# A fixed order at the begin of the joint stage, half 0's root one output tile earlier, and the last adaLN dots as GpSimd products summed by ScalarE

## The chip, the cores and the metric

The kernel runs on one core of a Trainium2 chip. The metric is the device time of one execution in microseconds, as a median of runs. TensorE is called PE in the profile, VectorE DVE, ScalarE ACT and GpSimd POOL; SP is the engine that issues most of the loads.

## The reference

One layer of a bidirectional encoder with 1024 positions and a width of 1024 (8 heads and 2 key heads of 64, window 128, 8 gMLP groups, feed-forward width 2816). Cut to what matters:

```python
mod = silu(c) @ w_ada + b_ada                 # adaLN
sh1, sc1, gt1, sh2, sc2, gt2 = split(mod, 6)
h = rmsnorm(x, norm1_g) * (1 + sc1) + sh1
u, v, q, k, va, gate_a, gate_b = split(h @ w_in)
v = rmsnorm(gelu(v), v_gain)
a_out = (gelu(u) * (w_s @ v + b_s)) @ w_a      # per chunk of 128 positions, per group
b_out = window_attention(q, k, va) @ w_b       # |t-s| <= 128, ALiBi, a sink per head
merged = sigmoid(gate_a) * a_out + sigmoid(gate_b) * b_out
x = x + gt1 * (merged @ w_o)
h2 = rmsnorm(x, norm2_g) * (1 + sc2) + sh2
f_gate, f_up = split(h2 @ w_ffn_in)
return x + gt2 * ((silu(f_gate) * f_up) @ w_ffn_out)
```

## The kernel before

Activations are kept with the width on the 128 partitions and positions along the row. The positions are two halves of 512. Every large product is made of three matmuls of rounded operands (high by high, low by high, high by low): `mm3` (L164) issues them, `unit` (L156) turns a raw weight tile into its high part `wh` (a cast on ACT) and its low part `wl` (a subtraction on DVE or POOL). One output tile of 128x512 takes 24 matmuls of 512 columns where the inner size is 1024. All operations go through a recording class whose call is L76, so every row of the profile has that line; `load` (L137) issues on SP and `store` (L140) on POOL. PE, DVE, ACT and POOL each run their own instructions in the order in which they stand; a scheduler chooses that order, except where `in_order[0]` is set: such instructions keep the order of the program (`tc.keep_in_program_order`). In feed-forward the order is all by hand (`tc.manual_schedule`).

The stages, in the order of time:

1. `half(hf)` (L732) for each half: q, k and v, the windowed attention, and the gMLP. The loop over `gp` (L1105) multiplies the position-mixing matrices with v into PSUM banks, and a `scalar_tensor_tensor` on DVE evicts each group into `ut` as u * (mixed + bias). Sixteen transposes of `ut` and a split into high and low parts (`gH`, `gL`) follow. The loop `for d in range(KT)` (L1157, eight output tiles) projects both branches by W_ab; for d below 2 the banks are multiplied with the gates right away, for the others stored.
2. In half 1 the same loop runs jobs ahead of the joint stage: `block_sums(k, part)` (L606) builds, from the normalised x of both halves, the blocks B11, B21, B22 and their sums and differences T1 to T4. The chunks it reads are a0, a1 (tiles `hs`) and b0, b1 (tiles `xs`), loaded by `block_load` (L586), b1 by an addition on POOL.
3. The joint stage, `for d in range(2, KT)` (L1239): the gates of both halves together by seven products in place of eight, `gate_step(d, i)` and `gate_evict(d, i)` with i from 0 to 6. Sums of weights are made by `gate_sums`, high and low parts by `gate_prep_a`, `_b`, `_c`, of which the last two return functions that issue the low part later. `held_projection` (L1211) is the last projection of half 1, kept back. `ada_half` (L542) computes one adaLN column as two dots of 512 on DVE. The order in this loop is the program's.
4. The output projection `for hf in range(2): for d in range(KT)` (L1344): W_o's product, an eviction to x1 = product * gt1 + x, the sum of squares `ss`, and a store of x1 to DRAM. In half 1, `col_rstd(sums[0], ...)` (L288) multiplies the squares of half 0 with ones on PE (tiles `at<-ones,ss`) and takes the root, `spread` (L295) spreads it over the partitions, and `mod2(i)` (L1336) loads x1 of half 0 back and makes the normalised, modulated h2 of tile i (tiles `mid` and `h`), which feed-forward multiplies first.
5. Feed-forward: groups f of hidden tiles, seven products each in later groups (step i), then the output products. `gain_dots(f, i)` (L1707) computes the eight last adaLN columns (gt2) from group EARLY = 6 on: it loads a row of w_ada, and two `scalar_tensor_tensor` with an accumulated sum on DVE make the dot.

The profile's tile names are those of the program without their numbers: `mm` and `at` are banks, `t` short-lived tiles, `raw` weights as loaded, `j` and `mid` the blocks' high and low parts among others.

## Time and profile before

| what | value |
|---|---|
| median of 3 runs | 1268.25 us (1266.0 to 1270.06) |
| the profiled execution | 1264.82 us |
| its span on the core | 1263.0 us |
| mean granted PE clock in it | 0.994 of full speed |

The span is the time from the first to the last instruction that the profile shows; 1.8 us of the execution lie outside it. In the timeline a row is: start, duration of the whole row, engine, line, operation, tile written and tiles read, shape, count, and in brackets the idle time of the engine before it and who ended it. In the table of windows a row holds the window, its length, the busy time and count of PE, PEld (the loading of weights into PE), DVE, ACT and POOL, then PE's granted clock, the busy share of the DMA engines and the GB/s. In the list of waits: the engine and tile that waited, what for, the sum, the number and the longest.

### The profile page before, as it was taken

The page shows a single profiled execution, that of the slowest core. Times are in us where ns is not written, and L with a number is a line of the kernel's source. Part 1 is how long each engine was busy: PE and PEld are TensorE (multiplying, and loading weights), DVE is VectorE, ACT ScalarE, POOL GpSimd, SP SyncE. Part 2 cuts the span into 40 slices and gives each one's busy share as a digit, 9 for nine tenths or more (in the row PEclk, how much of TensorE's full clock was granted, in tenths as well). Part 3 has the DMA queues.
Part 4 walks back from the last instruction along what each step waited for, and adds up shares of the span by engine and source line. Part 5 has one row for each costly group of instructions (what it writes and reads, how often), then busy time and mean ns, then how long its engine had stood idle before and what let it go on. Part 6 is the DMA issues. An engine that isn't in the chain of part 4 may idle for free.

```text
span 1263.0 us, 15661 instructions
## 1 busy us (share of the span) xinstructions
PE 1226.5 (97%) x5634; PEld 1013.4 (80%) x5634; DVE 917.3 (73%) x1548; ACT 577.7 (46%) x938; POOL 176.7 (14%) x218
## 2 busy tenths in 40 slices
PE   5999999999989999999899999999999999999998
PEld 4888888888877887788788887888788887888887
DVE  8998883588887799866798766777676676455646
ACT  5477864367866333434454332333333334443442
POOL 1223430013342000211100000000010000010001
PEclk9999999999999999999899999999999999999999
DMA  9722168421146466677702454565644549785542
GB/s 363 265 100 67 68 202 299 132 84 51 63 160 236 159 201 233 237 246 243 256 35 100 152 215 159 191 233 200 233 171 181 182 167 347 284 326 192 191 159 100
DMA packets 78688, 236.29 MB, mean 187 GB/s; under 512 B 9361, under 2 KB 9361, under 8 KB 72594
## 3 DMA queue, kind: packets, MB, share of 16 engines
q1 hardware_dynamic: 57602, 146.67, 33.3%
q0 software_dynamic: 17552, 82.32, 18.2%
q10 hardware_dynamic: 3456, 6.29, 1.3%
q8 instruction: 44, 0.72, 0.2%
q14 instruction: 34, 0.28, 0.1%
HBM read 177.58 MB, written 57.67 MB: 186 GB/s over the span
## 4 chain that ended last, share of the span: by engine, by line
PE 58%; issue 16%; DVE 13%; DMA 8%; ACT 4%; POOL 1%; SPq 0%; ACTq 0%; POOLq 0%; DVEq 0%
PE mm L76 31%; PE at L76 27%; DVE mid L76 4%; DVE wl L76 3%; DMA hs<-in_w_ada_dram 2%; DMA wS<-wo 2%; DMA wo<-in_w_out_dram 1%; ACT wh L76 1%; DVE hs L76 1%; DVE xs L76 1%; DMA mid<-in_w_ada_dram 1%; DMA hs<-x1d 1%; DVE t L76 1%; DVE ws L76 1%; ACT lb L76 1%
## 5 line engine op out<-in xcount | busy, mean ns | idle before, releaser
L76 DVE TENSOR_TENSOR wl<-raw,wh 128x1024 fp32r<-128x1024 f32 x141 | 171.9, 1221 | 90.8 <-ACT wh L76 88.6
L76 ACT CAST wh<-raw 128x1024 fp32r<-128x1024 f32 x155 | 162.4, 1051 | 149.9 <-PE at L76 47.7
L76 PE MATMUL mm<-mid,wh 128*128 128x512 f32 x696 | 215.5, 390 | 0.7 <-DVE mid L76 0.4
L76 PEld LDWEIGHTS mm<-mid,wh 128*128 128x128 f32 x696 | 130.3, 188 | 29.3 <-DVE mid L76 1.1
L76 PE MATMUL at<-j,wh 128*128 128x512 f32 x464 | 143.0, 389 | 0.0
L76 PE MATMUL mm<-mid,wl 128*128 128x512 f32 x348 | 135.4, 390 | 0.0
L76 PE MATMUL mm<-wh,h 128*128 128x512 f32 x384 | 128.9, 397 | 2.8 <-ACT h L76 2.8
L76 PEld LDWEIGHTS at<-j,wh 128*128 128x128 f32 x464 | 87.0, 188 | 18.2 <-ACT xs L76 0.2
L76 PE MATMUL at<-h,wh 128*128 128x512 f32 x288 | 91.3, 397 | 3.0 <-ACT h L76 2.8
L76 DVE TENSOR_TENSOR wl<-ws,wh 128x1024 fp32r<-128x1024 f32 (+1 forms) x55 | 62.0, 1128 | 43.0 <-ACT wh L76 43.0
L76 PE MATMUL mm<-j,wh 128*128 128x512 f32 x288 | 89.9, 394 | 0.9 <-ACT wh L76 0.9
L76 PE MATMUL at<-j,wl 128*128 128x512 f32 x232 | 90.4, 390 | 0.2 <-DVE wl L76 0.2
L76 PEld LDWEIGHTS mm<-wh,h 128*128 128x128 f32 x384 | 71.2, 188 | 17.9 <-ACT h L76 4.1
L76 PE MATMUL mm<-h,wh 128*128 128x512 f32 x272 | 84.6, 392 | 0.0
L76 ACT CAST wh<-ws 128x1024 fp32r<-128x1024 f32 (+1 forms) x55 | 53.6, 974 | 63.8 <-DVE ws L76 54.3
L76 PEld LDWEIGHTS mm<-mid,wl 128*128 128x128 f32 x348 | 65.3, 188 | 14.1 <-DVE wl L76 0.3
L76 PE MATMUL mm<-wl,h 128*128 128x512 f32 x192 | 75.1, 391 | 0.4 <-DVE wl L76 0.4
L76 PEld LDWEIGHTS at<-h,wh 128*128 128x128 f32 x288 | 54.8, 191 | 15.9 <-ACT h L76 3.2
L76 PEld LDWEIGHTS mm<-j,wh 128*128 128x128 f32 x288 | 54.3, 189 | 12.4 <-ACT wh L76 1.3
L76 ACT ACTIVATE xs<-xs 128x512 f32<-128x512 f32 x21 | 13.3, 633 | 105.3 <-DVE xs L76 105.3
L76 DVE TENSOR_TENSOR ol<-raw,oh 128x1024 fp32r<-128x1024 f32 x30 | 36.7, 1224 | 32.6 <-ACT oh L76 32.5
L76 PEld LDWEIGHTS mm<-h,wh 128*128 128x128 f32 x272 | 50.6, 188 | 10.4
(279 smaller groups left out, 2580.3 us busy)
## 6 DMA issues: line engine op xcount, KB each, us to landing
raw<-in_w_gate_dram SPq DMA_DIRECT2D x28, 512.0 KB, 4.0
tA<-hid POOLq DMA_DIRECT2D x11, 1024.0 KB, 5.0
tB<-hid POOLq DMA_DIRECT2D x11, 1024.0 KB, 5.0
wo<-in_w_out_dram POOLq DMA_DIRECT2D x22, 512.0 KB, 6.1
wS<-wo POOLq DMA_DIRECT2D x11, 1024.0 KB, 5.3
raw<-wS SPq DMA_DIRECT2D x44, 256.0 KB, 3.0
raw<-tB SPq DMA_DIRECT2D x44, 256.0 KB, 3.4
raw<-in_w_out_dram SPq DMA_DIRECT2D x33, 256.0 KB, 5.1
```

The costliest lines, as they stand in the source:

```text
L76: ins = f(*args, **kw)
```

## The change

Six edits:

- **The gMLP's evictions** of half 1 keep the program's order, and so do the projections of tiles 6 and 7 and the jobs behind tiles 0, 6 and 7 of half 1.
- **The blocks**: the negation of B22 goes from the first part of `block_sums` to the end of the second. `block_sums(3, 1)` is no job any more: it stands in the joint stage. At d = 2 the order there becomes step 0, its eviction, `held_projection`, `block_sums(3, 1)`, step 1; it was step 0, eviction, step 1, `held_projection`.
- **`ada_half`** in the joint stage stands behind the low part of `gate_prep_c` in the step's first third, and no longer at the step's end.
- **Half 0's root** stands at the begin of output tile 1 of half 1 and not of tile 2, `spread` at the begin of tile 2 and not within tile 3; `mod2` runs at tiles 2 to 7 as 0; 1; 2, 3; 4; 5, 6; 7 where it ran at 3 to 7 as 0, 1; 2; 3, 4; 5; 6 and 7 behind the last eviction.
- **`gain_dots`**: each of the sixteen fused products with sum on DVE becomes a `tensor_tensor` on POOL (steps 2 and 4) and an activation with `accum_out` on ACT at the next odd step; the row is loaded at step 6 and no longer at 5.
- The store of silu(c) is written behind block 5 of attention and not behind block 0; on POOL it stands in the same place in both kernels.

DVE at the end of half 1, before. `mid_2667` is `ut`, `at_3656` to `at_3683` the gMLP's banks, `mid_2671` is `gL`; `xs_3747`, `xs_3743`, `hs_3745` are the block's chunks b1, b0, a0; `t_760` and `t_761` the gates of projection tile 0; `wl_3802` the low part of W_ab's weights of tile 2 (two stretches, the eviction of the transposes between them left out):

```order
L76 TENSOR_TENSOR xs_3620<-at_3615,xs_3620 64x512
L76 TENSOR_TENSOR xs_3747<-xs_3747,xs_3743 128x512
L76 SCALAR_TENSOR_TENSOR mid_2667<-at_3656,cc,mid_2667 128x4x64 x2
L76 SCALAR_TENSOR_TENSOR mid_2667<-at_3665,cc,mid_2667 128x4x64 x2
L76 SCALAR_TENSOR_TENSOR mid_2667<-at_3674,cc,mid_2667 128x4x64 x2
L76 SCALAR_TENSOR_TENSOR mid_2667<-at_3683,cc,mid_2667 128x4x64 x2
```

```order
L76 TENSOR_TENSOR xs_3743<-xs_3743,hs_3745 128x512
L76 SCALAR_TENSOR_TENSOR t_760_3692<-t_760_3692,mm_3751 128x512
L76 SCALAR_TENSOR_TENSOR j_3784<-xs_3747,nsh,j_3783 128x512
L76 SCALAR_TENSOR_TENSOR mid_3838<-hs_3745,mod,mid_3837 128x512
L76 TENSOR_TENSOR xs_3747<-xs_3747,hs_3745 128x512
L76 SCALAR_TENSOR_TENSOR mid_3841<-hs_3749,mod,mid_3840 128x512
L76 SCALAR_TENSOR_TENSOR t_761_3694<-t_761_3694,mm_3765 128x512
L76 TENSOR_TENSOR j_3788<-xs_3743,j_3787 128x512
L76 TENSOR_TENSOR t_760_3692<-t_760_3692,t_761_3694 128x512
L76 TENSOR_TENSOR j_3793<-xs_3747,j_3792 128x512
L76 TENSOR_TENSOR wl_3802<-raw_3734,wh_3801 128x1024
```

DVE at the same place with the change (`wl_3800` is that low part), from the gMLP's evictions to the weights, without the eviction of the transposes:

```order
L76 TENSOR_TENSOR xs_3620<-at_3615,xs_3620 64x512
L76 SCALAR_TENSOR_TENSOR mid_2667<-at_3656,cc,mid_2667 128x4x64 x2
L76 SCALAR_TENSOR_TENSOR mid_2667<-at_3665,cc,mid_2667 128x4x64 x2
L76 SCALAR_TENSOR_TENSOR mid_2667<-at_3674,cc,mid_2667 128x4x64 x2
L76 SCALAR_TENSOR_TENSOR mid_2667<-at_3683,cc,mid_2667 128x4x64 x2
```

```order
L76 SCALAR_TENSOR_TENSOR t_760_3692<-t_760_3692,mm_3751 128x512
L76 SCALAR_TENSOR_TENSOR t_761_3694<-t_761_3694,mm_3765 128x512
L76 TENSOR_TENSOR t_760_3692<-t_760_3692,t_761_3694 128x512
L76 TENSOR_SCALAR nsh<-mod 128x8
L76 TENSOR_TENSOR xs_3747<-xs_3747,xs_3743 128x512
L76 TENSOR_TENSOR xs_3743<-xs_3743,hs_3745 128x512
L76 SCALAR_TENSOR_TENSOR j_3784<-xs_3747,nsh,j_3783 128x512
L76 TENSOR_TENSOR xs_3747<-xs_3747,hs_3745 128x512
L76 TENSOR_TENSOR hs_3749<-xs_3747,hs_3749 128x512
L76 TENSOR_TENSOR j_3788<-xs_3743,j_3787 128x512
L76 TENSOR_TENSOR j_3793<-xs_3747,j_3792 128x512
L76 TENSOR_TENSOR wl_3800<-raw_3734,wh_3799 128x1024
```

The sum of b1 and b0 moved from ahead of the four pairs of evictions to a place behind the gates of tile 0, and with it the whole block, so that the gates of tile 0 now stand ahead of every sum of it and all of it ahead of the weights.

DVE at the begin of the joint stage, before: the block's last sums, the weights' sums (`raw`), and the low part of step 1's weights (`wl_4121`):

```order
L76 TENSOR_TENSOR xs_4057<-xs_4057,hs_4052 128x512
L76 TENSOR_TENSOR j_3788<-xs_4004,j_3787 128x512
L76 TENSOR_TENSOR raw_4013<-raw_4013,t_841_4070 128x512
L76 TENSOR_TENSOR j_3793<-xs_4057,j_3792 128x512
L76 TENSOR_TENSOR raw_4013<-raw_4013 128x512
L76 TENSOR_TENSOR hs_4060<-xs_4057,hs_4060 128x512
L76 TENSOR_TENSOR wl_4121<-raw_4015,wh_4120 128x1024
L76 TENSOR_TENSOR t_849_4124<-t_841_4070,t_848_4123 128x512
L76 SCALAR_TENSOR_TENSOR h_3849<-hs_4060,nsh,h_3848 128x512
```

The same place with the change (`wl_4119` is step 1's low part):

```order
L76 TENSOR_TENSOR xs_4055<-xs_4055,hs_4050 128x512
L76 TENSOR_TENSOR j_3788<-xs_4004,j_3787 128x512
L76 TENSOR_TENSOR j_3793<-xs_4055,j_3792 128x512
L76 TENSOR_TENSOR wl_4119<-raw_4013,wh_4118 128x1024
L76 TENSOR_TENSOR raw_4011<-raw_4011,t_841_4070 128x512
L76 TENSOR_TENSOR raw_4011<-raw_4011 128x512
L76 TENSOR_TENSOR t_849_4122<-t_841_4070,t_848_4121 128x512
L76 TENSOR_TENSOR hs_4058<-xs_4055,hs_4058 128x512
L76 SCALAR_TENSOR_TENSOR h_3847<-hs_4058,nsh,h_3846 128x512
```

The low part of step 1's weights moved up by three rows, ahead of two sums of weights and the last block's sum. On PE the 12 matmuls of `held_projection` stand between steps 0 and 1 with the change, and behind step 1 before.

PE in the output projection of half 1, before: `mm_5461` is output tile 0, `mm_5497` tile 1, `mm_5539` tile 2, `at_5540` the product of ones with half 0's squares `ss_5077`:

```order
L76 MATMUL mm_5497<-j_5118,wh_5455 128x512
L76 MATMUL mm_5497<-j_5117,wl_5456 128x512
L76 MATMUL at_5540<-ones,ss_5077 128x1 x4
L76 MATMUL mm_5539<-j_5115,wh_5491 128x512
L76 MATMUL mm_5539<-j_5116,wh_5491 128x512
```

The same with the change (the product is `at_5498`):

```order
L76 MATMUL mm_5461<-j_5118,wh_5399 128x512
L76 MATMUL mm_5461<-j_5117,wl_5400 128x512
L76 MATMUL at_5498<-ones,ss_5077 128x1 x4
L76 MATMUL mm_5497<-j_5115,wh_5455 128x512
L76 MATMUL mm_5497<-j_5116,wh_5455 128x512
```

The four matmuls with ones moved from behind tile 1 to behind tile 0, 24 matmuls earlier. On DVE and ACT the sums of squares of half 0 keep their order.

```diff
--- before.py
+++ after.py
@@ -581,7 +581,7 @@
     nsh = const.tile([P, 16], F32, tag="nsh", name="nsh")[:, :8]
     blk = {}
 
-    chunk = {}
+    chunk, kinds = {}, []
 
     def block_load(k, name):
         if k < 4:
@@ -629,8 +629,6 @@
             low1()
             block_load(k + 1, "b0")
             low2()
-            for x in blk["B22"]:
-                A.activation(x[:, k, :], x[:, k, :].bitcast(F32), AF.Copy, scale=-1.0)
             return
         if k < 3:
             low = b11()
@@ -643,6 +641,8 @@
         block_load(k + 1, "b1")
         low()
         block_load(k + 1, "a1")
+        for x in blk["B22"]:
+            A.activation(x[:, k, :], x[:, k, :].bitcast(F32), AF.Copy, scale=-1.0)
 
     raws, gunits, acc, held = {}, {}, {}, []
 
@@ -1060,7 +1060,7 @@
                 x_square(s + 1)
             if hf == 0 and s == 7:
                 x_rstd()
-            if hf == 0 and s == 0:
+            if hf == 0 and s == 5:
                 store(silu_d, silu_c)
             normalise(sc[0], sc[2], den)
             if s == 0:
@@ -1110,6 +1110,7 @@
                 wc = slice(g * P, (g + 1) * P)
                 mm3(pg[:, e * 256 : (e + 1) * 256], (ws[0][:, wc], ws[1][:, wc]),
                     (vH[:, g, :], vL[:, g, :]), True, True)
+            in_order[0] = hf == 1
             for e in range(2):
                 g = 2 * gp + e
                 uu = ut[:, :, g * HD : (g + 1) * HD]
@@ -1117,6 +1118,7 @@
                     out=uu, in0=pg[:, e * 256 : (e + 1) * 256].rearrange("p (n d) -> p n d", d=HD),
                     scalar=bsT[:, g : g + 1], in1=uu, op0=ALU.add, op1=ALU.mult,
                 )
+            in_order[0] = False
         def gate_act(pg):
             sg = tmp()
             A.activation(sg, pg, AF.Tanh, scale=0.5)
@@ -1147,15 +1149,15 @@
         else:
             apool_ctx.close()
             jpools.append(ffn_ctx.enter_context(pool("j", 6, reuse_waits="tile")))
-            kinds = (lambda: midt(F32R, 4)), (lambda: jt(F32R, 4)), hid
+            kinds[:] = (lambda: midt(F32R, 4)), (lambda: jt(F32R, 4)), hid
             blk["B22"] = (hH[1], hL[1])
             for x in ("b0", "a0", "b1", "a1"):
                 block_load(0, x)
             jobs.extend((2 * k + p, lambda k=k, p=p: block_sums(k, p, kinds))
-                        for k in range(4) for p in range(2))
+                        for k in range(4) for p in range(2) if k + p < 4)
 
         for d in range(KT):
-            in_order[0] = d < 2
+            in_order[0] = d < 2 or hf == 1 and d > 5
             if 0 < d < KT - 1:
                 wab.append(unit(None, V, abr.pop(0)))
                 if d + 2 + hf < KT:
@@ -1194,9 +1196,10 @@
             if d < 2:
                 V.tensor_tensor(ms[0], ms[0], ms[1], op=ALU.add)
                 store(md[hf][d], ms[0])
-            in_order[0] = False
+            in_order[0] = hf == 1 and (d < 1 or d > 5)
             while jobs and jobs[0][0] <= d:
                 jobs.pop(0)[1]()
+            in_order[0] = False
             if hf == 0:
                 ada_next(d < 1)
                 if d > 5:
@@ -1240,8 +1243,9 @@
         if d == 2:
             gate_step(d, 0)
             gate_evict(d, 0)
+            held_projection()
+            block_sums(3, 1, kinds)
             gate_step(d, 1)
-            held_projection()
             low_c = gate_prep_c(d)
             gate_evict(d, 1)
             low_c()
@@ -1261,7 +1265,6 @@
             gate_evict(d, 5)
             low_b()
             low_s()
-            ada_half("hs")
             continue
         gate_step(d, 0)
         gate_evict(d, 0)
@@ -1269,6 +1272,7 @@
         low_c = gate_prep_c(d)
         gate_evict(d - 1, 6)
         low_c()
+        ada_half("hs" if not last else None)
         if not last:
             gate_load(d + 1)
         gate_step(d, 1)
@@ -1315,7 +1319,6 @@
             if d in (3, 4, 5):
                 ada_half("hs")
             low_s()
-            ada_half("hs" if d < KT - 2 else None)
     in_order[0] = False
     for k in (4, 5, 7):
         m_split(m0, k)
@@ -1357,15 +1360,15 @@
             load(xk, x_rows(hf, d))
             pw = mm_bank()
             for k in range(KT):
+                if hf == 1 and (d, k) == (1, 0):
+                    col_rstd(sums[0], NT, rcol[2])
                 if hf == 1 and (d, k) == (2, 0):
-                    col_rstd(sums[0], NT, rcol[2])
-                if hf == 1 and (d, k) == (3, 3):
                     rb = spread(rcol[2], NT)
                 kc = slice(k * P, (k + 1) * P)
                 mm3(pw, (wo[0][:, kc], wo[1][:, kc]),
                     (m[k // 4][0][:, k % 4, :], m[k // 4][1][:, k % 4, :]), k == 0, k == KT - 1)
             if hf == 1:
-                for i in {3: (0, 1), 4: (2,), 5: (3, 4), 6: (5,), 7: (6,)}.get(d, ()):
+                for i in {2: (0,), 3: (1,), 4: (2, 3), 5: (4,), 6: (5, 6), 7: (7,)}.get(d, ()):
                     mod2(i)
             x1 = tmp() if hf == 0 else x1B[d // 4][:, d % 4, :]
             V.scalar_tensor_tensor(out=x1, in0=pw, scalar=mod[:, GT1 + d : GT1 + d + 1], in1=xk,
@@ -1385,7 +1388,6 @@
                 if 0 < d < 7:
                     ada_next(False)
             if hf == 1 and d == KT - 1:
-                mod2(d)
                 early.append(unit(None, V, raw1))
         in_order[0] = False
         sums.append(ss)
@@ -1702,29 +1704,29 @@
                             for x in "hl"]
             split2(raws[n], *ready[n])
 
-    again = []
+    again, dots = [], []
 
     def gain_dots(f, i):
         if f == EARLY and i == 0:
             again.extend(stream("hs") for _ in range(2))
             for j in range(2):
                 dma(again[j], silu_d[:, j * 512 : (j + 1) * 512])
-        if not ada_queue:
-            return
-        if f >= EARLY and i == 5:
+        if f >= EARLY and ada_queue and i == 6:
             again[2:] = [tmp(), tmp()]
             for j in range(2):
                 dma(again[2 + j], w_ada2[ada_queue[0][0] - GT1][:, j * 512 : (j + 1) * 512])
-        if f > EARLY and i in (3, 4):
-            j = int(i == 4)
+        if dots and i % 2:
+            dots.pop(0)()
+        if f > EARLY and ada_queue and i in (2, 4):
+            j = i // 2 - 1
             col = ada_queue[0][0]
             part = sm(16, "part")[:, :1]
-            V.scalar_tensor_tensor(out=again[2 + j], in0=again[2 + j], scalar=1.0, in1=again[j],
-                                   op0=ALU.mult, op1=ALU.mult,
-                                   accum_out=part if j else acc_mod[:, col : col + 1])
+            row = again[2 + j]
+            G.tensor_tensor(row, row, again[j], op=ALU.mult)
+            dots.append(lambda: A.activation(row, row, AF.Copy,
+                                             accum_out=part if j else acc_mod[:, col : col + 1]))
             if j:
-                added(acc_mod[:, col : col + 1], part)
-                ada_end(col)
+                dots.append(lambda: (added(acc_mod[:, col : col + 1], part), ada_end(col)))
                 ada_queue.pop(0)
 
     with tc.manual_schedule():
```

## The prediction

> **What bounds the kernel now.** I read the page's busy shares first, then the waits of the matmul engine alone, in two windows, and then the timeline around each wait that is long enough to matter.
>
> ```profile
> span 1263.0 us, 15661 instructions
> PE 1226.5 (97%) x5634; PEld 1013.4 (80%) x5634; DVE 917.3 (73%) x1548; ACT 577.7 (46%) x938; POOL 176.7 (14%) x218
> ```
>
> TensorE (PE) is busy for 1226.5 of 1263.0 us, and the change leaves the number of matmuls as it is. So what can be won is the 36.5 us in which PE stands still, and the time in which it runs at a lower clock. Where it waits, between 340 and 640 us and then after 640 us (line, what it waits for: sum, times, longest, in us):
>
> ```profile
> PE at L76 <- DVE mid L76: 4.8, 2, 4.0
> PE at L76 <- ACT h L76: 2.8, 1, 2.8
> PE mm L76 <- DVE wl L76: 1.7, 2, 1.3
> PE mm L76 <- ACT wh L76: 0.9, 1, 0.9
> ```
>
> ```profile
> PE mm L76 <- DVE wl L76: 1.6, 1, 1.6
> PE at L76 <- DVE xs L76: 0.8, 1, 0.8
> ```
>
> Four waits carry the first window, and three places hold them: the transposes behind the gMLP gate of half 1, the joint stage's begin, and the begin of feed-forward. After 640 us there is little to win. Each of the three places is followed by a window in which the granted clock (the column PEclk, behind the five engines) is 0.50. The windows below are 350 to 357, 401 to 408, 620 to 627 us, two of feed-forward, and the stretch of half 1's projections.
>
> ```profile
> 350.28:353.69 3.41, 0.00 (x0) 0.00 (x0) 3.38 (x3) 1.67 (x3) 3.41 (x2) 1.00 0.08 18
> 353.69:357.10 3.41, 3.11 (x15) 3.07 (x16) 3.41 (x9) 1.46 (x4) 1.46 (x1) 0.50 0.61 196
> 401.48:404.90 3.42, 1.72 (x6) 1.15 (x7) 3.42 (x6) 2.57 (x5) 0.00 (x0) 1.00 0.64 264
> 404.90:408.30 3.40, 3.40 (x9) 2.64 (x9) 0.67 (x2) 0.00 (x0) 0.00 (x0) 0.50 0.81 259
> ...
> 619.90:626.70 6.80, 6.21 (x18) 4.93 (x19) 4.15 (x6) 5.75 (x7) 1.04 (x1) 0.50 0.43 155
> 710.00:830.00 120.00, 118.04 (x518) 96.78 (x517) 82.57 (x128) 40.57 (x56) 8.82 (x17) 1.00 0.55 200
> 830.00:960.00 130.00, 129.21 (x570) 106.68 (x569) 95.69 (x151) 43.20 (x60) 11.22 (x21) 1.00 0.57 204
> 353.00:403.00 50.00, 47.77 (x210) 39.42 (x210) 45.90 (x68) 34.87 (x55) 15.18 (x16) 0.97 0.61 205
> ```
>
> The window behind a wait runs 3.4 us at half clock, so it does 1.7 us of work; a wait that goes takes these 1.7 us with it, and a new wait may bring them.
>
> **A, the gate's evictions in written order.**
>
> ```profile
> 350.12 2.82 DVE L76 TENSOR_TENSOR xs<-xs,xs 128x512 f32<-128x512 f32 x1 [3.50 <-POOL xs L76]
> 352.97 3.23 DVE L76 SCALAR_TENSOR_TENSOR mid<-at,cc,mid 128x256 f32<-128x256 f32 x8
> 350.04 5.12 POOL L76 TENSOR_TENSOR wl<-raw,wh 128x1024 fp32r<-128x1024 f32 x2
> 353.99 3.45 PE L76 MATMUL at<-ident,mid 128*128 128x128 f32 x16 [4.05 <-DVE mid L76]
> ```
>
> VectorE (DVE) is idle for 3.50 us on a sum of a joint-stage block whose other operand GpSimd (POOL) writes; that sum then takes 2.82 us; only then come the eight evictions, while PE waits 4.05 us for them. In the new order the block's sum stands behind the evictions. The banks come until 349.95 (353.99 less 4.05); the last pair then needs 2 x 0.40 us (3.23 over 8), so 0.85 us of the wait stays. Gone: 4.05 - 0.85 + 1.7 (the half clock) = 4.9, and 0.3 of the eight being begun while banks still come: **-5.2 us**, bounds -3.2 (the clock falls all the same) and -5.75 (all goes).
>
> The same rows show why the sum was slow: 2.82 us beside POOL's subtraction, where one of this size takes 0.68 alone (below), while the evictions, with one operand from a bank, ran 0.40 apart beside the same subtraction. The Trainium skill, "SBUF — State Buffer", section "Who interferes with whom", has it as an exclusive lock on a pair of ports, taken by a DVE instruction with two inputs from SBUF against a GpSimd one that reads SBUF; these rows agree. It speaks against the last part of the change, F.
>
> **B, a new wait two projection tiles later.** In the fixed order DVE has to take the gates of projection tile 0 (two products with a bank, and their sum) before it goes to the first block's sums. Tile 0 is 24 matmuls at 0.227 us, 5.44 us, as its neighbours are.
>
> ```profile
> 357.20 0.72 PE L76 MATMUL mm<-mid,wh 128*128 128x512 f32 x2
> 402.05 0.68 DVE L76 TENSOR_TENSOR hs<-xs,hs 128x512 f32<-128x512 f32 x1
> 402.65 1.21 DVE L76 TENSOR_TENSOR wl<-raw,wh 128x1024 fp32r<-128x1024 f32 x1
> 571.29 0.74 DVE L76 SCALAR_TENSOR_TENSOR t<-mm,mod,xs 128x512 f32<-128x512 f32 x1
> 572.96 1.05 ACT L76 CAST wh<-raw 128x1024 fp32r<-128x1024 f32 x1 [2.92 <-DMA raw<-in_w_o_dram]
> 573.91 0.63 ACT L76 ACTIVATE t<-t 128x512 f32<-128x512 f32 x1
> ```
>
> Tile 0 begins at 357.20 now; without A's 5.2 us it begins at 352.0 and ends at 357.4. Behind that end stand on DVE a product of 0.74 (as at 571.29), a sum and two block sums 0.60 apart (402.05 to 402.65), a product of 0.74 and another sum; the block's cast on ScalarE (ACT), taken like the 0.63 row, and the weights' cast of 1.05 follow behind it: 357.4 + 0.74 + 3 x 0.60 + 0.74 + 0.60 + 0.63 = 361.9 for the begin of the weights' cast. One short instruction and the handovers between the two engines are not in this; I put them at 0.1 to 0.7 in all, an estimate, so the cast of tile 2's weights ends at 363.1 to 363.7. PE, after tiles 0 and 1, wants it at 352.0 + 2 x 5.44 = 362.9. Then four matmuls (0.9 us) need the cast alone; DVE's subtraction of 1.21 us has one more sum before it and ends about 0.6 us behind them. I take 0.8 + 0.6, since every handover adds: **+1.4 us**, bounds 0 (the weights' cast slips in earlier) and +3.1 (the clock falls too).
>
> On that clock there is a rule. In 401.48 to 404.90 PE did 1.72 of 3.42 us, with waits of 0.88 and 1.29, and got 0.50 in the next window. The Trainium skill, "TensorE: Matmul & The Clock Gate", section "HAM oscillation — how this bites in real kernels", asks only that no gap without work be over about 3.4 us. By that rule B would stay at 1.4; by the row it could be 3.1. The row decides that shorter gaps can do it, and 3.1 stays as the bound.
>
> **C, the joint stage's begin.**
>
> ```profile
> 401.90 0.74 PE L76 MATMUL mm<-j,wh 128*128 128x512 f32 x2 [0.88 <-ACT wh L76]
> 403.92 0.50 PE L76 MATMUL mm<-j,wl 128*128 128x512 f32 x1 [1.29 <-DVE wl L76]
> ```
>
> PE waits 0.88 and 1.29 us for step 1's weights, and the half clock of 404.90 to 408.30 adds 1.7. The change puts the 12 matmuls of the held projection ahead of step 1, 12 x 0.227 = 2.72 us of cover, and lets the low part of the weights go three rows earlier on DVE, 3 x 0.60 = 1.8 us. Against it: PE arrives 3.8 us earlier (A and B), and DVE, 45.90 of 50 us busy between 353 and 403, has to come forward as well. It gets 2.14 (2.82 less 0.68) from A's sum, and it has 4.1 us of idle time, of which I count about 0.4: PE gains 1.3 us on it. The cover of 4.5 less 1.3 is over the 2.17 needed. The two dots that stand later or earlier by three rows in every joint step (1.4 us beside steps without a wait of PE) are part of this order and cost nothing. **-3.9 us**, bounds 0 and -3.9.
>
> **D, half 0's root at tile 1.** The matmuls of ones against the sum of squares stand behind tile 0 instead of behind tile 1.
>
> ```profile
> 571.57 0.61 PE L76 MATMUL mm<-j,wh 128*128 128x512 f32 x2
> 577.02 0.95 PE L76 MATMUL at<-ones,ss 128*128 128x1 f32 x8
> 574.04 1.23 DVE L76 TENSOR_TENSOR wl<-raw,wh 128x1024 fp32r<-128x1024 f32 x1 [2.01 <-ACT wh L76]
> 575.18 0.69 DVE L76 TENSOR_TENSOR ss<-ss,t 128x512 f32<-128x512 f32 x1
> ```
>
> Now PE comes to them at 577.02, when the last sum has been there since 575.87 (575.18 + 0.69). One tile earlier it comes at 571.57, and the sum isn't earlier: the last square (573.91) stands on ACT behind the weights' cast, which waits 2.92 us for a transfer, and the last addition on DVE behind the subtraction of 574.04, which waits for that cast. Neither engine's order around it changes. All of tile 1 is queued behind the waiting matmul: 575.87 - 571.57 = 4.3 us, and the half clock after it 1.7: **+6.0 us**. Bounds: without the detour through the weights the sum would be there at 571.29 + 0.74 + 0.63 + 0.69 = 573.35, 1.8 us late, so +1.8; a second half-clock window gives +7.7. The root itself and the spread of it, a tile earlier too, have nobody waiting for them.
>
> **E, half 0's modulation earlier.**
>
> ```profile
> 616.97 0.50 PE L76 MATMUL at<-h,wh 128*128 128x512 f32 x1 [0.26 <-DVE h L76]
> 620.49 1.58 PE L76 MATMUL at<-h,wh 128*128 128x512 f32 x2 [2.79 <-ACT h L76]
> 619.72 0.72 ACT L76 ACTIVATE h<-mid,mod 128x512 fp32r<-128x512 f32 x1 [1.42 <-DVE mid L76]
> ```
>
> Feed-forward's first product waits for the last two tiles of the normalised half 0: 0.26 + 2.79 us, and 6.8 us at half clock follow, in which PE is busy for 6.21, worth 3.1. The last tile is now issued before the eviction of output tile 7 and not after it, and the others a tile earlier, which puts 5.44 us of matmuls ahead of the need. Half a microsecond I leave for the last one: 3.05 + 3.1 - 0.5: **-5.6 us**, bounds -1.0 (DVE, which now has two such tiles beside one output tile, is late) and -6.2.
>
> **F, the dots.** Sixteen fused products with sums leave DVE; sixteen products come to POOL and sixteen sums to ACT.
>
> ```profile
> L76 DVE SCALAR_TENSOR_TENSOR t<-t,hs 128x512 f32<-128x512 f32 x16 | 10.9, 683 | 0.0
> L76 DVE DVE_READ_ACCUMULATOR t<-t,hs 128x1 f32 x16 | 1.3, 82 | 0.0
> ```
>
> ```profile
> 348.79 1.30 POOL L76 TENSOR_TENSOR xs<-h,h 128x512 f32<-128x512 f32 x1
> 776.75 0.69 DVE L76 TENSOR_TENSOR hid<-hid 128x512 f32<-128x512 f32 x1 [3.81 <-DMA wS<-wo]
> ```
>
> DVE loses 10.9 + 1.3 = 12.2 us of work. Almost none of it is on the path: PE is busy 118.04 of 120 and 129.21 of 130 us, and the one longer wait of PE there, the 1.6 us for wl above, stands behind a DVE sum that waits 3.81 us for a transfer. POOL gets 16 x 1.30 = 20.8 us, 0.53 us more per dot than DVE is freed of (1.30 less 0.77), if each product shuts DVE out for its whole length; DVE has 37.4 us without work in the first of these windows and 34.3 in the second, which hide that. ACT's sums, of about the length of the 0.63 row, fall on an engine at 34% (40.57 of 120). The store of silu(c) moves in the code only. **-1.0 us**, bounds -2.4 (the waits over 640 us of the second waits fence) and +3.
>
> **The sum.** -5.2 + 1.4 - 3.9 + 6.0 - 5.6 - 1.0 = -8.3. The profiled execution took 1264.82 us (1.8 outside its span): 1256.5. The median of the runs, 1268.25, stands 3.4 us above that execution, so on its scale I forecast 1259.9, say **1260**.
>
> **Rivals.** *R1, the root's wait is mostly hidden*: the last square overtakes the cast, D is +1.8 and not +6.0: 1260 - 4.2 = 1256. For it speaks that ACT only waits for a transfer; against it, that the order on ACT and DVE there is unchanged. *R2, DVE is the bound between 353 and 403*: at 92% busy it does not come forward, C is 0, and 1.3 us of A comes back as a longer wait at the joint stage's begin: 1260 + 5.2 = 1265. For it: the share. Against it: the idle 3.50 us and the stretched 2.82 us both lie ahead of this stretch, so DVE starts it earlier. *R3, slower: POOL's products shut out DVE's subtractions in feed-forward.* All sixteen on the path, at 1.30 us, give +20.8 where I have -1.0: 1260 + 21.8 = 1282. The kernel is slower beyond 0.3% from 1272.1 - 1261 = 11.1 us of it, 9 of the 16 products. For it: the 2.82 us of A. Against it: a step of 12 matmuls is 2.72 us, in which DVE works 69% or 1.87 us, less the dot that leaves; 1.87 - 0.77 + 1.30 = 2.40 still fits. The change may also not do what it says at E, where a late DVE leaves 4.6 of the 5.6 us: 1264.6.
>
> **How the numbers follow.** Forecast 0.48, R1 0.15, R2 with E's failure 0.23, R3 0.14. What a measurement can tell from no change is 0.3%, 3.8 us: faster is below 1264.4, slower above 1272.1. Forecast and R1 are faster nearly whole, and a little of R2: 0.65. The rest of R2 and the forecast's upper end: 0.22. R3 with the upper bounds of B and D: 0.13. The range runs from R1 with the better bounds of A, B, E and F (1252) to R2 with the upper bounds of B and D and a little of F's (1270); it leaves out R3 and little else.
>
> **What would show it.** A: no wait near 350 us, and no window of 0.50. B: a wait of PE for tile 2's cast or low part about 10 us later. C: step 1's matmuls without a wait behind the held projection's. D: `at<-ones,ss` with some 4 us of idle time for DVE's ss and a 0.50 window after it; without it R1 holds. E: no wait for h at feed-forward's first product. F: DVE subtractions of 1.21 us stretched beyond 2 us beside POOL's products, and new waits for wl after 800 us, would be R3. The forecast is wrong if the mean clock falls below 0.994, or if waits for DVE appear between 360 and 403 us that I do not have.

## The result and the profile after

The changed kernel takes 1265.72 us (median of 20 runs, 1260.78 to 1269.63); the kernel before, run beside it, 1266.37 us (20 runs, 1263.6 to 1270.34). The ratio is 0.9992, 95% interval 0.9981 to 1.0004: no difference. The forecast was 1260 us and faster; the time lies inside the range of 1252 to 1270 us, but the gain is not there.

The profiled execution must be read with one caution. It took 1269.63 us, the slowest of its 20 runs, while that of the kernel before, 1264.82 us, lies 1.5 us below its median. The two traces differ by 4.9 us of span where the medians differ by 0.65, so a place is judged below by several traces of the same order of work.

The page of the changed kernel, the span and the busy shares:

```profile
span 1267.9 us, 15678 instructions
PE 1228.1 (97%) x5634; PEld 1013.0 (80%) x5634; DVE 919.5 (73%) x1516; ACT 586.0 (46%) x970; POOL 198.9 (16%) x234
```

TensorE does the same matmuls. Its waits in the changed kernel, from 340 to 420 us, 420 to 560, 560 to 640, and 640 to 1000 (one fence each; sum, times, longest):

```profile
PE mm L76 <- ACT wh L76: 0.6, 1, 0.6
PE mm L76 <- POOL wl L76: 0.5, 1, 0.5
PE at L76 <- DVE wl L76: 0.5, 1, 0.5
PE mm L76 <- DVE wl L76: 0.3, 1, 0.3
```

```profile
PE at L76 <- DVE mid L76: 4.1, 3, 1.5
```

```profile
PE at L76 <- DVE ss L76: 5.3, 2, 4.2
```

```profile
PE mm L76 <- ACT xs L76: 3.6, 3, 1.7
PE mm L76 <- DVE wl L76: 2.9, 2, 2.3
```

The waits of 4.0, 1.3 and 0.9 us around 350 and 402 us are gone, as forecast, and so is the 2.8 us for h. Three groups stand in their place: 4.1 us in the joint stage, where the kernel before has 1.1; 5.3 us for sums of squares, where it has none; and 6.5 us in feed-forward, where it has 2.8. The rows of B's wait, of the first wait in the joint stage, of the root and of the begin of feed-forward:

```profile
363.20 1.20 PE L76 MATMUL mm<-mid,wh 128*128 128x512 f32 x4 [0.61 <-ACT wh L76]
364.66 0.50 PE L76 MATMUL mm<-mid,wl 128*128 128x512 f32 x1 [0.27 <-DVE wl L76]
451.01 2.33 PE L76 MATMUL at<-j,t 128*128 128x512 f32 x9 [1.44 <-DVE mid L76]
573.32 1.59 PE L76 MATMUL at<-ones,ss 128*128 128x1 f32 x8 [4.20 <-DVE ss L76]
623.25 1.02 PE L76 MATMUL at<-ones,ss 128*128 128x1 f32 x8 [1.06 <-DVE ss L76]
```

The windows of the changed kernel (gate, joint stage, root, begin of feed-forward, feed-forward):

```profile
349.00:352.40 3.40, 2.85 (x20) 2.20 (x19) 2.28 (x6) 3.40 (x7) 3.40 (x3) 1.00 0.02 5
352.40:355.80 3.40, 3.40 (x16) 2.80 (x15) 3.22 (x6) 1.44 (x3) 1.77 (x1) 1.00 0.71 186
440.00:500.00 60.00, 55.93 (x243) 44.81 (x242) 53.32 (x98) 19.74 (x27) 4.85 (x9) 1.00 0.64 217
573.30:576.70 3.40, 3.38 (x13) 3.00 (x14) 2.13 (x4) 2.52 (x3) 2.05 (x2) 0.55 0.85 286
576.70:580.10 3.40, 3.40 (x10) 2.63 (x9) 1.07 (x1) 0.00 (x0) 0.49 (x1) 0.50 0.61 233
620.00:627.00 7.00, 5.93 (x26) 4.56 (x25) 5.13 (x7) 5.08 (x8) 1.58 (x2) 0.85 0.23 80
710.00:830.00 120.00, 115.17 (x505) 94.09 (x504) 84.37 (x109) 40.90 (x64) 17.88 (x23) 1.00 0.53 193
830.00:960.00 130.00, 128.20 (x565) 105.41 (x564) 93.58 (x135) 50.33 (x82) 23.76 (x31) 1.00 0.58 207
```

There is no window of 0.50 behind the gate any more. Behind the root the clock stands at 0.50 for two windows one after the other, from 573.66 to 580.49 us; the row with 0.55 begins a little before them.

To compare many traces I add up, by stage, how much further apart matmul starts stand than is usual for their size (0.227 us from start to start for 512 columns, 0.174 for 384, 0.120 for 256, 0.109 for 128, 0.213 for one). Waits and lower clock both show in it. In us, by the stage's time in the trace:

| trace | 340–362 (A) | 362–380 (B) | 380–420 (C) | 440–510 (joint) | 560–600 (D) | 600–640 (E) | 760–1000 (F) |
|---|---|---|---|---|---|---|---|
| before | 5.8 | 0.0 | 4.9 | 0.9 | -0.7 | 6.7 | 3.8 |
| changed | 1.0 | 1.4 | 1.1 | 5.3 | 8.3 | 2.2 | 8.0 |
| u_ada | 1.0 | 1.5 | 1.7 | -0.1 | 7.6 | -0.3 | 7.5 |
| ada_mid | 1.0 | 1.5 | 1.1 | 1.1 | 4.7 | 0.4 | 7.6 |
| ada_load_after | 1.0 | 1.4 | 1.5 | -0.1 | 6.9 | 2.0 | 6.8 |
| u_dots | 1.0 | 1.5 | 1.2 | 3.1 | 7.6 | 0.9 | 5.2 |
| dve_products | 1.0 | 1.4 | 1.2 | 3.6 | 7.2 | 0.0 | 4.3 |
| u_root | 1.0 | 1.4 | 1.2 | 2.8 | -0.1 | 7.4 | 8.6 |
| root_late | 1.0 | 1.5 | 1.2 | 3.7 | -0.2 | 3.7 | 8.0 |
| square_first | 1.0 | 1.4 | 1.2 | 3.6 | 2.7 | -0.4 | 8.2 |
| order_only | 1.0 | 1.4 | 1.2 | -0.1 | 0.2 | 8.1 | 4.6 |
| order_mod | 1.0 | 1.5 | 1.1 | 0.2 | 0.1 | 6.4 | 4.5 |
| gate_only | 1.0 | 0.0 | 6.0 | -0.1 | -0.4 | 6.3 | 5.6 |
| best_late | 1.0 | 1.4 | 1.1 | -0.1 | -0.8 | 3.6 | 2.5 |
| best_square | 1.0 | 1.5 | 1.2 | 1.1 | 1.7 | 5.5 | 2.1 |
| best_free | 1.0 | 0.0 | 2.9 | 0.5 | -0.6 | 2.7 | 1.7 |

The first 340 us, which no kernel here changes, vary from 23.8 to 26.7 in the same sum: that much of a trace is chance.

The clock over all runs says something that the two traces hide. Its median over the 20 runs of the changed kernel is 0.9965, and that of the kernel before, in the runs beside the experiments, 0.993. By an estimate from these figures (0.0035 of 1266 us) the changed kernel loses about 4.4 us less to the half clock, and still takes the same time: on balance, what it loses anew it loses by waiting.

### The profile page after: what moved, and what is told of

The parts are those of the page before. It is cut to its first block, busy times and chain, and to the rows that moved or that the text cites. A ratio compares the mean times of both kernels' runs of the same rounds, so it can differ in the third digit from the quotient of the medians.

```text
span 1267.9 us, 15678 instructions
## 1 busy us (share of the span) xinstructions
PE 1228.1 (97%) x5634; PEld 1013.0 (80%) x5634; DVE 919.5 (73%) x1516; ACT 586.0 (46%) x970; POOL 198.9 (16%) x234
## 4 chain that ended last, share of the span: by engine, by line
PE 72%; DVE 12%; DMA 8%; issue 4%; ACT 4%; SPq 0%; POOL 0%; ACTq 0%; DVEq 0%; POOLq 0%
PE at L76 37%; PE mm L76 35%; DVE mid L76 3%; DVE wl L76 3%; DMA raw<-in_w_o_dram 2%; ACT wh L76 2%; DMA raw<-in_w_ga_dram 1%; DMA mid<-in_w_ada_dram 1%; DVE ws L76 1%; DMA hs<-md 1%; DMA hs<-x1d 1%; DVE hid L76 1%; DMA wS<-wo 1%; DVE xs L76 1%; ACT lb L76 1%
## 5 line engine op out<-in xcount | busy, mean ns | idle before, releaser
L76 DVE TENSOR_TENSOR wl<-ws,wh 128x1024 fp32r<-128x1024 f32 (+1 forms) x55 | 66.0, 1200 | 44.3 <-ACT wh L76 44.3
L76 PE MATMUL mm<-j,wl 128*128 128x512 f32 x144 | 57.3, 398 | 1.1 <-DVE wl L76 1.1
```

The costliest lines, as they stand in the source:

```text
L76: ins = f(*args, **kw)
```

## The experiments

Fourteen kernels ran, each timed against the kernel before. Ratios are to that kernel, with 95% intervals; "faster than the changed kernel" compares ratios, and 0.001 is 1.27 us. The intervals reach 0.0012 to each side for the changed kernel and about 0.0014 for the others, so the difference of two ratios is uncertain by about 0.0018, 2.3 us: 3.5 us or more is clear of that, 1.3 to 1.9 us is not.

### One part taken back, or the first two edits alone

**u_ada**: the joint stage's dots at the step's end.

```diff
-        ada_half("hs" if not last else None)
...
             low_s()
+            ada_half("hs" if d < KT - 2 else None)
```

> The changed kernel with one edit taken back: in the joint stage the two adaLN dots stand at the step's end again and not behind the low part of gate_prep_c. Theory (the moved dots cost time: in the profile of the changed kernel TensorE waits 1.6, 1.3 and 1.6 us near 451, 471 and 493 us for an eviction that DVE reaches two dots later): 4 to 5 us faster than the changed kernel, and those three waits are gone. Rival (the joint stage is simply reached earlier and the waits come with that, wherever the dots stand): no difference beyond 1 us, the waits stay.

1261.46 us, ratio 0.9959 (0.9944 to 0.9974): 0.0033, 4.2 us faster than the changed kernel. TensorE has no wait at all between 420 and 560 us, against 4.1 us. The move of the dots costs 4 us.

**u_dots**: feed-forward's dots as before.

```diff
-            G.tensor_tensor(row, row, again[j], op=ALU.mult)
-            dots.append(lambda: A.activation(row, row, AF.Copy, accum_out=...))
...
+            V.scalar_tensor_tensor(out=again[2 + j], ..., accum_out=...)
```

> The changed kernel with the dots of feed-forward taken back to fused products with sums on DVE. Theory (GpSimd's products shut DVE out: eight DVE operations of feed-forward last 0.8 to 2.7 us longer in the profile of the changed kernel, and TensorE waits some 4 us more between 780 and 855 us): 4 to 6 us faster than the changed kernel, no stretched DVE operation, waits there as in the kernel before (about 2 us). Rival (those waits follow late transfers and differ from run to run): within 1.5 us.

1263.56 us, 0.9981 (0.9967 to 0.9995): 1.4 us faster than the changed kernel, just under the rival's bound and far from 4 to 6. The runs alone do not show this difference. The traces do: 5.2 in feed-forward against 8.0, and no stretched operation on DVE. The direction is the theory's; the size is smaller.

**u_root**: root, spread and modulation of half 0 back at their places.

```diff
-                if hf == 1 and (d, k) == (1, 0):
+                if hf == 1 and (d, k) == (2, 0):
                     col_rstd(sums[0], NT, rcol[2])
...
```

> The changed kernel with half 0's root, its spread and the modulation back at their places (root at output tile 2, modulation at tiles 3 to 7 and behind the last). Theory (the root's wait of 4.2 us and about 3.3 us of half clock are paid, and 4.4 us at the begin of feed-forward are won): 2.5 to 3.5 us faster than the changed kernel, the wait for the sum of squares gone, and the waits of 0.3 and 2.8 us for h back. Rival (the earlier modulation is worth more than the root's wait costs, as with the prediction's best bound): 1 to 4 us slower.

1263.88 us, 0.9977 (0.9963 to 0.9991): 1.9 us faster than the changed kernel, less than the 2.5 to 3.5 expected and not clear of the uncertainty. So the part that the prediction put at +6.0 - 5.6 costs about 2 us net, and is at least no gain. The table has both halves: D falls from 8.3 to -0.1, E rises from 2.2 to 7.4.

**order_only**: the kernel before with the first two edits alone. (The store of silu(c) is written as in the changed kernel too.)

```diff
+            in_order[0] = hf == 1
             for e in range(2):
...
+            held_projection()
+            block_sums(3, 1, kinds)
             gate_step(d, 1)
-            held_projection()
```

> The kernel before with the first two edits alone: the fixed order at the gMLP's evictions and the projections, and the joint stage's begin (held projection and the block's last sums ahead of step 1). Theory (the terms A, B and C of the prediction hold): 6 to 8 us faster than the kernel before, and faster than the changed kernel by about as much. Rival (what is won at 350 and 402 us is lost at later waits of the joint stage, since DVE sets its pace): under 3 us.

1258.12 us, 0.9927 (0.9910 to 0.9944): 9.2 us faster than the kernel before, a little over the 6 to 8 expected. Terms A, B and C hold, and nothing later takes them back. The four runs add up: 9.2 won, then 4.2, 1.4 and 1.9 us lost by the dots' move, feed-forward's dots and the root, leaves a gain of 1.7, and 1.0 (0.9992) is measured.

### What in each part costs the time

**ada_load_after**: the dots stay where the change puts them; the loads of the next row go behind the loads of the weights.

```diff
-        ada_half("hs" if not last else None)
+        ada_half(None)
         if not last:
             gate_load(d + 1)
+            ada_half_load("hs")
```

> The changed kernel with the joint stage's dots at their changed place on DVE, but the load of the next column's row on SP behind the loads of the next weights and not ahead of them. Theory (the dots themselves, 1.8 us of DVE work ahead of the eviction, delay the bank for which TensorE waits): the three waits near 450, 471 and 492 us stay at 1 us or more, within 1.5 us of the changed kernel. Rival (SP's queue: the row's load waits for the dots and holds up the weights' loads behind it, so casts and everything behind them come late): the waits go and the time falls by 3 to 4 us, as with the dots at the step's end.

1260.93 us, 0.9959 (0.9944 to 0.9974): 4.2 us faster than the changed kernel, like u_ada, and the three waits are gone. The theory that the dots' own time is the cost falls; it is SP's queue. The queue in the changed kernel and then in this one (a row's length is the time from the first to the last issue in it):

```profile
428.24 16.22 SPq L137 DMA_DIRECT2D hs<-in_w_ada_dram  x6
444.58 0.36 SPq L137 DMA_DIRECT2D raw<-in_w_ga_dram  x1
```

```profile
423.00 14.53 SPq L137 DMA_DIRECT2D hs<-in_w_ada_dram  x6
437.62 0.38 SPq L137 DMA_DIRECT2D raw<-in_w_ga_dram  x1
```

The last two of the six row loads wait until the moved dots are done with the old rows (DVE begins these dots at 442.80), and in the changed kernel the weights of the next step stand behind them: they are issued at 444.58, where u_ada issues them at 441.92 and ada_load_after at 437.62 (TensorE is 0.9 and 0.5 us later in these two traces at that place). The cast of these weights on ScalarE, in the changed kernel:

```profile
451.26 1.05 ACT L76 CAST wh<-raw 128x1024 fp32r<-128x1024 f32 x1 [6.50 <-DMA raw<-in_w_ga_dram]
```

In ada_load_after the cast of the same weights begins at 445.21 and waits for nothing. This cast is too late to have caused the wait at 451; that one hangs on the step before, where the cast begins at 429.16 after 3.44 us of waiting and in ada_load_after at 426.17 without any. DVE's idle time behind such casts from 410 to 510 us, in the changed kernel and in ada_load_after:

```profile
DVE wl L76 <- ACT wh L76: 7.7, 11, 2.2
```

```profile
DVE wl L76 <- ACT wh L76: 2.7, 7, 0.7
```

DVE is busy for 53.32 of 60 us here; it does not catch up 5 us, and an eviction (`mid<-xs,at`) then reaches TensorE's bank 1.4 us late in three steps. That last link is read from the rows, not tried by itself.

**ada_mid**: the dots behind the eviction of step 1.

```diff
-        ada_half("hs" if not last else None)
         if not last:
             gate_load(d + 1)
         gate_step(d, 1)
         gate_evict(d, 1)
+        ada_half("hs" if not last else None)
```

> The changed kernel with the joint stage's two adaLN dots one eviction later, behind the eviction of step 1 and not ahead of the loads and step 1. Theory (the dots cost time because they stand ahead of the eviction of step 1, for whose bank TensorE waits): the three waits near 451, 471 and 493 us go, 4 us faster than the changed kernel, like the dots at the step's end. Rival (any place in the step's first third is too early for DVE, whose work is spread over the step): the waits move to the next step of products and stay at 1 us or more each.

1262.93 us, 0.9982 (0.9966 to 0.9998): the three waits are gone (1.1 us are left in the table's column, none of them for an eviction at those places), but the time is 1.3 us below the changed kernel's and not 4. Why it isn't more stays open. In it the row loads stand behind the weights' loads too, so it does not tell dots from loads; ada_load_after does.

**dve_products**: the products on DVE, the sums on ScalarE.

```diff
-            G.tensor_tensor(row, row, again[j], op=ALU.mult)
+            V.tensor_tensor(row, row, again[j], op=ALU.mult)
```

> The changed kernel with the sixteen products of feed-forward's dots as tensor_tensor on DVE and not on GpSimd; ScalarE's sums stay. Theory (GpSimd's products shut out DVE): as with the whole edit taken back, 2 us faster than the changed kernel, no stretched DVE operation between 700 and 1000 us. Rival (the sums on ScalarE hold up its evictions, and TensorE waits for those): no faster than the changed kernel, and the waits for ACT xs near 790, 810 and 850 us stay.

1260.19 us, 0.9964 (0.9947 to 0.9981): 3.5 us faster than the changed kernel. ScalarE's sums are still there and the waits for ACT are not; TensorE's only wait from 640 to 1000 us:

```profile
PE mm L76 <- DVE wl L76: 2.2, 1, 2.2
```

So GpSimd's products are the cost. In the changed kernel, on DVE, GpSimd and ScalarE around 806 us:

```profile
806.55 3.96 DVE L76 TENSOR_TENSOR wl<-ws,wh 128x1024 fp32r<-128x1024 f32 x1 [0.51 <-ACT wh L76]
810.44 0.68 DVE L76 TENSOR_TENSOR t<-at,t 128x512 f32<-128x512 f32 x1
```

```profile
806.89 2.54 POOL L76 TENSOR_TENSOR t<-t,hs 128x512 f32<-128x512 f32 x2
```

```profile
811.15 0.63 ACT L76 ACTIVATE t<-t 128x512 f32<-128x512 f32 x1 [4.63 <-DVE t L76]
811.69 0.57 ACT L76 COPY xs<-mm 128x512 f32<-128x512 f32 x1
```

```profile
812.30 0.73 PE L76 MATMUL mm<-mid,wh 128*128 128x512 f32 x2 [0.75 <-ACT xs L76]
```

The subtraction takes 3.96 us, its usual 1.23 and the 2.54 of two products that ran into it; the sum behind it is late, ScalarE waits 4.63 us for that sum, and the copy that frees TensorE's bank stands behind; TensorE waits 0.75 us for it. It is not one instruction alone: from 700 to 1040 us, each of the seven traces with GpSimd's products has eight or nine DVE operations that last 0.5 us or more beyond the median of their kind, 12 to 17 us in sum, and none of the nine other traces has any. The mean of such subtractions in feed-forward (700 to 1000 us), in the changed kernel and in dve_products:

```profile
L76 DVE TENSOR_TENSOR wl<-ws,wh 128x1024 fp32r<-128x1024 f32 x31 | 42.0, 1354 | 31.5 <-ACT wh L76 31.5
```

```profile
L76 DVE TENSOR_TENSOR wl<-ws,wh 128x1024 fp32r<-128x1024 f32 x32 | 39.2, 1226 | 28.7 <-ACT wh L76 28.7
```

A mean that is 0.13 us longer hides that two of the 31 lost nearly all of it: 2.7 us at 806.55 and 1.2 us at 843.81.

**root_late**: the root 21 matmuls later, the spread likewise.

```diff
-                if hf == 1 and (d, k) == (1, 0):
+                if hf == 1 and (d, k) == (1, 7):
                     col_rstd(sums[0], NT, rcol[2])
-                if hf == 1 and (d, k) == (2, 0):
+                if hf == 1 and (d, k) == (2, 7):
                     rb = spread(rcol[2], NT)
```

> The changed kernel with the root's matmuls 21 matmuls later, ahead of the last three of output tile 1, and the spread ahead of the last three of tile 2; the modulation stays as changed. Theory (the root's wait and the half clock behind it are what the earlier root costs, and both depend only on where TensorE meets the sum of squares): no wait for it, 1.00 as granted clock, 6 to 8 us faster than the changed kernel, the begin of feed-forward as in the changed kernel. Rival (the wait moves to the spread or to the modulation, because the root's way over DVE and GpSimd is as long as before): under 3 us, with a wait of TensorE for the root's column or for h.

1261.04 us, 0.9962 (0.9948 to 0.9976): 3.8 us faster than the changed kernel, between the theory's 6 to 8 and the rival's 3. The wait at the root is gone (the row of `at<-ones,ss` at 572.25 has no wait and D is -0.2). But the begin of feed-forward now waits, for the sum of squares of half 1:

```profile
612.65 0.50 PE L76 MATMUL at<-h,wh 128*128 128x512 f32 x1 [0.29 <-ACT h L76]
613.44 0.50 PE L76 MATMUL at<-h,wh 128*128 128x512 f32 x1 [0.28 <-DVE h L76]
615.64 1.02 PE L76 MATMUL at<-ones,ss 128*128 128x1 f32 x8 [1.48 <-DVE ss L76]
```

E is 3.7 where the traces with the root's wait have -0.3 to 2.2. One reading is that the time in which TensorE stands at the root lets DVE and ScalarE get ahead for the begin of feed-forward, so that the two terms are not independent. Nine traces fit it (with 4.7 to 8.3 lost at the root E is at most 2.2, with nothing lost there 3.7, 3.6 and 2.7), one pair does not: square_first has 2.7 and -0.4, best_square 1.7 and 5.5. What sets E beyond this stays open.

**square_first**: the root at tile 1 as changed, the last square and its addition ahead of the next weights' cast and subtraction (in program order).

```diff
+                in_order[0] = hf == 1 and d < 2
                 wo_next = unit(w_o[d + 1])
...
+            in_order[0] = in_order[0] or hf == 0 and d == 7
             V.scalar_tensor_tensor(out=x1, ...
```

> The changed kernel with the last square of half 0 and its addition ahead of the cast and the subtraction of output tile 2's weights on ScalarE and DVE; the root stays at tile 1. Theory (the sum of squares is late only because its square stands behind a cast that waits for a transfer): the wait at the root falls from 4.2 to about 1 us and no window of half clock follows, 5 to 7 us faster than the changed kernel. Rival (the eviction ahead of the square, or the square itself, is what is late): the wait stays above 3 us and the time within 2 us of the changed kernel's.

1261.37 us, 0.9964 (0.9951 to 0.9977): 3.5 us faster than the changed kernel; the wait is what was expected and the time is won by half. The row of the root, and the window behind it:

```profile
567.36 1.05 PE L76 MATMUL at<-ones,ss 128*128 128x1 f32 x8 [0.98 <-DVE ss L76]
```

```profile
568.40:571.80 3.40, 3.40 (x10) 2.63 (x10) 1.39 (x2) 1.99 (x3) 1.44 (x2) 0.51 0.97 352
```

4.2 us of wait become 0.98: the sum of squares was late because its square stood behind a cast that waits for a transfer. Still, one window of half clock follows. What the window ahead of it holds is told in the last section.

**order_mod**: the first two edits, the modulation earlier, the root where it was.

```diff
-                for i in {3: (0, 1), 4: (2,), 5: (3, 4), 6: (5,), 7: (6,)}.get(d, ()):
+                for i in {3: (0, 1), 4: (2, 3), 5: (4,), 6: (5, 6), 7: (7,)}.get(d, ()):
```

> The kernel with the first two edits alone, and the modulation of half 0 at output tiles 3 to 7 as 0, 1; 2, 3; 4; 5, 6; 7, the last ahead of the last eviction, with the root left at tile 2 and its spread within tile 3 as in the kernel before. Theory (the gain at the begin of feed-forward comes from the modulation's place and needs no earlier root): no wait for h at 615 us, no wait for the sum of squares at 570, 4 to 6 us faster than the first two edits alone, about 1253 us. Rival (two modulated tiles beside one output tile overload DVE without the earlier root): within 1.5 us of the first two edits alone, with a wait for h or for the evictions.

1258.17 us, 0.9949 (0.9933 to 0.9965): no faster than order_only (0.9927, the intervals overlap). The rival holds. TensorE's waits at the begin of feed-forward:

```profile
611.59 0.50 PE L76 MATMUL at<-h,wh 128*128 128x512 f32 x1 [1.17 <-ACT h L76]
612.38 0.50 PE L76 MATMUL at<-h,wh 128*128 128x512 f32 x1 [0.28 <-DVE h L76]
614.86 1.37 PE L76 MATMUL at<-ones,ss 128*128 128x1 f32 x8 [1.74 <-DVE ss L76]
```

Against order_only the longer wait for h fell from 2.8 to 1.2 us, and one of 1.7 us for the squares came. It may be that DVE, without an earlier root, has the same work in five tiles, so that the last tile's square is late instead; no run tries that.

**gate_only**: the kernel before with the gMLP's evictions of half 1 in written order and nothing else.

```diff
+            in_order[0] = hf == 1
             for e in range(2):
...
+            in_order[0] = False
         def gate_act(pg):
```

> The kernel before with one edit alone: the gMLP's evictions of half 1 in written order. Theory (terms A and C are separate): the wait of 4.0 us and the half clock near 350 us go, which is 4.5 to 5 us of matmul time there, no wait for tile 2's weights near 363 us, and the joint stage's begin at 402 us waits as before or 1 to 2 us longer, because TensorE comes earlier: 3 to 5 us faster than the kernel before. Rival (what is won at 350 us is waited for in full at 402 us, DVE being busy in between): within 1.5 us of the kernel before.

1261.91 us, 0.9975 (0.9964 to 0.9986): 3.2 us faster than the kernel before, as expected. A is 1.0, B is 0.0, and the joint stage's begin waits longer than before (0.9 and 1.3 there):

```profile
PE mm L76 <- ACT wh L76: 2.5, 1, 2.5
PE mm L76 <- DVE wl L76: 0.9, 1, 0.9
```

### Versions put together from the parts

**best_late**: the first two edits, the dots of the joint stage at the step's end, feed-forward's products on DVE with ScalarE's sums, root and spread as in root_late.

```diff
-        ada_half("hs" if not last else None)
...
+            ada_half("hs" if d < KT - 2 else None)
...
-            G.tensor_tensor(row, row, again[j], op=ALU.mult)
+            V.tensor_tensor(row, row, again[j], op=ALU.mult)
...
-                if hf == 1 and (d, k) == (1, 0):
+                if hf == 1 and (d, k) == (1, 7):
...
```

> The first two edits, the joint stage's dots at the step's end as before, feed-forward's products on DVE with ScalarE's sums, and the root and spread as in the run with the late root. If the parts add up as they have (about 8 us below the kernel before by the first two edits, 4 us at the begin of feed-forward, none lost at the root): 1252 to 1255 us, a ratio to the kernel before of 0.989 to 0.992. If the begin of feed-forward gives nothing net: as the first two edits alone, 0.993.

1251.91 us (1250.88 to 1253.22), 0.9897 (0.9878 to 0.9915): 13.0 us faster than the kernel before. The parts add up: 9.2 (order_only), 2.1 (dve_products against u_dots) and 1.9 (root_late against u_root) are 13.2.

**best_square**: the same with the root at tile 1 and square_first's order.

```diff
-                if hf == 1 and (d, k) == (1, 7):
+                if hf == 1 and (d, k) == (1, 0):
...
+                in_order[0] = hf == 1 and d < 2
                 wo_next = unit(w_o[d + 1])
...
```

> The same with the root at tile 1 as changed and the last square ahead of the cast. If the parts add up: 1252 to 1256 us, 0.989 to 0.992. If the weights of output tile 2 become late because their cast and subtraction stand behind the square and the root: a wait of TensorE for wh or wl at tile 2, and 0.993 or more.

1253.0 us, 0.9907 (0.9887 to 0.9928): no different from best_late within the intervals, with waits for wl of 1.8 us in sum between 560 and 700 us, which best_late does not have there.

**best_free**: best_late with the first job of half 1 left to the scheduler.

```diff
-            in_order[0] = hf == 1 and (d < 1 or d > 5)
+            in_order[0] = hf == 1 and d > 5
```

> The fastest version so far (the first two edits, dots of the joint stage as before, feed-forward's products on DVE, late root) with the first job of half 1's projections left to the scheduler's order. Theory (term B: the wait of about 1.4 us for tile 2's weights comes from that fixed order): no wait near 363 us, 1 to 1.5 us faster than that version. Rival (the block's sums then come late for the joint stage, as in the run with the gMLP's order alone, where TensorE waited 2.5 us for step 1's weights): the wait near 363 us goes and one of the same size or more comes at 397 us.

1251.75 us, 0.9888 (0.9871 to 0.9905): the same time. B's 1.4 us are gone and 1.8 us (2.9 against 1.1) come in the next column, at 386 and 400 us. The rival holds in kind: whichever goes first, block or weights, the other is late.

## Why the prediction was wrong, step by step

- **A (-5.2)**: right, -4.8 in the trace (5.8 to 1.0). The half clock went with the wait.
- **B (+1.4)**: right, +1.4 in the table, as a wait for the cast of tile 2's weights, one for their low part, and no half clock.
- **C (-3.9)**: right, -3.8 in the trace (4.9 to 1.1). DVE did come forward; R2, which has DVE as the bound of that stretch, did not happen. gate_only shows what happens without the reordering: 6.0 us.
- **The dots of the joint stage (0)**: this step failed. It said that two dots moved by three rows "cost nothing" because TensorE has no wait beside them. They cost 4.2 us (u_ada, ada_load_after). The working counted the instructions on DVE and left out that the same call issues two loads, and that the move sets them ahead of the weights' loads in SP's queue.
- **D (+6.0)**: the mechanism was right and the wait too (4.2 us, forecast 4.3), the half clock was mis-sized: the wait was followed by two windows and not one, and against before (-0.7) the stage lost 9.0 us in this trace and 5.4 to 8.3 in five others with the same root. The bound of +7.7, a second such window, had this case, though four of the six traces lie above it. In five of the six the second window came. There the root's own eight matmuls of one column stand mostly in the first window (1.25 of its 3.41 us in the changed kernel); in ada_mid, with one window, 0.62 us of them do.
- **E (-5.6)**: -4.5 in the changed kernel's trace and up to -7 in others with the root's wait (from 6.7 to between -0.3 and 2.2). Without that wait E is worth -3 to -4 (root_late, best_late and best_free leave 3.7, 3.6 and 2.7), since the sum of squares of half 1, not named in the prediction, is late next. Together D and E cost 1.9 us (u_root) where the sum had 0.4; the difference is within the uncertainty of the runs.
- **F (-1.0)**: the step failed in its sign. The idle time of DVE, 37.4 and 34.3 us in two windows, was taken as cover, but a product comes at one place in a step, and what is behind it there waits. Between 760 and 1000 us the seven traces with GpSimd's products lose 6.8 to 8.6 us, the five with fused dots 3.8 to 5.6 and the four with products on DVE 1.7 to 4.3. In runs it is 1.4 us against the fused dots, which is not clear of the uncertainty, and 3.5 us against products on DVE, which is. R3's mechanism was the true one, at a fraction of its price: GpSimd's products hold DVE up, 3.96 us where 1.23 is usual, and the stretched subtractions that the prediction names as R3's sign came (the new waits are for ScalarE's copies, though, and not for wl). The Trainium skill, "SBUF — State Buffer", section "Who interferes with whom", says that a DVE instruction with two inputs from SBUF contends with a GpSimd one that reads SBUF; 3.96 us beside 2.54 agree.

The three failures, 4.2 + (1.9 - 0.4) + (1.4 + 1.0), are 8.1 us. A, B and C together gave 1.5 us more than the sum had (9.2 against 7.7). That accounts for 6.6 us of what is missing, 8.3 forecast less 0.65 measured; the last us is within the uncertainty of the runs. That the time lies inside the range is luck: it is R2's 1265, but not by R2's cause.

Neither of the two signs by which the prediction would have called itself wrong came: the mean clock did not fall (0.994 in the trace, 0.9965 over the runs), and of the waits for DVE between 360 and 403 us there is only B's. The failures lay in places that it had put at nothing or taken as covered.

## What to carry to other kernels

When a call moves, list what it issues on every queue, loads first: a load that waits for its buffer holds up the loads behind it, as the weights' loads in the joint stage were. Average idle time is no cover for an engine that shuts another out; look at the one instruction that it meets and at what stands behind it. And an edit that removes one wait and sets another may be more or less than the sum of the two: measure them together and apart.
